# All 22 units of the up projection in seven block products, four of them begun in an order written by hand; a tail laid out anew; a modulation vector turned earlier

## The chip, the cores and the metric

The kernel runs on one core of a Trainium2 chip. A core has five engines that work side by side and wait for one another by semaphores: TensorE (PE: matrix products into the accumulator memory PSUM), VectorE (DVE), ScalarE (ACT), GpSimd (POOL) and SyncE (SP), which issues most transfers between HBM and the on-chip memory SBUF. The metric is the device time of one execution in microseconds (us); less is better.

## The reference, cut to what matters

One layer of a diffusion backbone over 1024 tokens of width 1024: a combined projection, neighbourhood attention, two-way retention, gated merge, an output projection and a residual; then a gated MLP with a short convolution along the tokens. The change is in the MLP, at its entrance and at the kernel's end:

```python
x = x + g1 * _merge(o_na, o_ret, xga, xgb, w_proj_na, w_proj_ret, w_out)
hx2 = _rmsnorm(x, norm2_g) * (1.0 + sc2) + sh2
u = hx2 @ w_up                                   # 1024 x 5632
u = sum(up[:, i:i + n] * conv_w[i] for i in range(3)) + conv_b
a, val = split(u, 2)
x = x + g2 * ((silu(a) * val) @ w_down)          # 2816 x 1024
return _rmsnorm(x, final_norm_g)
```

Everything is float32. The kernel makes a float32 product of three matmuls: each operand is split into a rounded high part (ACT, a copy to the type float32r) and the rest (DVE, a subtraction), and high by high, high by low and low by high are added in PSUM.

## The kernel before, in words

**Units.** The up projection's 5632 columns are worked as 22 units. A unit is one block of 128 gate columns together with its 128 value columns, over all 1024 tokens: a 2 x 2 grid of output blocks (two branches by two halves of 512 tokens), summed over 1024 inputs, which are two groups of four blocks of 128. Done plainly (`up`, with `mm_a`), a unit takes 2 branches x 2 halves x 8 input blocks x 3 = 96 matmuls of 128x512. Done in seven block products (class `Seven`, for this stage its subclass `Up`), it takes 7 x 4 x 3 = 84: the weights' 2 x 2 blocks a11, a12, a21, a22 and four sums s1 to s4 of them are multiplied by B11, B21, B22 and four sums T1 to T4 of the moving blocks (the products T2 and T1 with s2 and s1, T3 with s3, T4 with a22), and DVE combines the products. In the kernel before, the first two units (`PLAIN = 2`) are plain and the other 20 go by seven products. `open3` (L1417) issues the matmuls of the seven-product units, `chain` (L117 to L119) those of the plain ones.

**Where the operands come from.** `out_proj(tb)` computes 128 tokens of the residual stream into `xr`; `norm_out(tb)` turns `xr` on PE (row `tp`), applies scale and shift (the vector `a2` and a part of `col`) and leaves high and low parts: for the first half of the tokens in `h2a`, for the second in `h2h` and `h2l`. For the tokens of the second half it also forms the four sums T1 to T4 with the first half's rows (`vo`, read back from `d_h`) and stores them in `d_t`. They are loaded again and split into the tiles `T` (16 splits of 128x512), which the seven-product units need. Eight blocks of tokens are done one after another; `norm_out` of a block comes behind `out_proj` of the next.

**Weights.** Each weight block is loaded into one of 12 raw buffers (`ur`; `raw` ahead of that stage) and split into one of six buffers `wc`. For the first units of the seven products the sums s1 to s4 are made in HBM by adding DMAs that POOL issues during the gates stage and `out_proj` (`block_sums`, `puts`, into `d_s`: six units, 48 DMAs); for later units POOL adds them in SBUF.

**What sets the order.** Outside blocks under `tc.manual_schedule()` a scheduler orders each engine's instructions; inside them they stand as written. Each engine works its own list in order. In the seven-product stage the units are interleaved: sorted by 7 x unit + 2 x step, so two units are open at a time. `conv` (three taps, silu, product) follows a unit's last combination on ACT and DVE. The down projection (`y` banks) ends the program; its last four bank results are finished one after another under a manual order (`finish`: factor on POOL, scaling on ACT and DVE, two stores).

**The second modulation vector.** Behind the 16 `pn` products, `col[:, 16:48]` (shift, scale and gates) is added to its bias, turned on PE into `tpa`, copied by ACT to `arow` and stored in `d_ada`, from where gate rows are read back.

Of the kernel before, what the change touches and what calls it, by code (L numbers as in the profile page):

```python
# [40 lines left out]
def tile_hybrid_layer(ctx, tc: tile.TileContext, io, dbg=None):  # L41
# [17 lines left out]
    d_s = dram.tile([6, 4, P, 512], F32, name="d_s")  # L59
# [490 lines left out]
    NH, PLAIN, PRE = NF // 2, 2, 6  # L550
# [28 lines left out]
    def up_jobs():  # L579
        return weight_jobs(d_s, [io["w_up"][seq[PLAIN + n]] for n in range(PRE)])  # L580
# [838 lines left out]
    class Seven:  # L1419
# [14 lines left out]
        def prod(self, bank, a, c, first, last):  # L1434
            w = wtile()
            split(w[:, 0], w[:, 1], a)
            for k, (xh, xl) in enumerate(self.moving(c)):
                open3(bank, w[:, 0, k * P : (k + 1) * P], w[:, 1, k * P : (k + 1) * P], xh, xl, first and k == 0, last and k == KH - 1)
# [97 lines left out]
    hs = None  # L1536
    hs = [hx_sums(k) for k in range(KH)]
# [9 lines left out]
    for n, (db, half) in enumerate(order):  # L1547
# [25 lines left out]
    pool.tensor_tensor(col[:, 16:48], col[:, 16:48], bcol[:, 16:48], ALU.add)  # L1573
    a2 = cpool.tile([P, KB], F32, name="a2")
    pool.tensor_scalar(a2, col[:, 32:40], 1.0, None, ALU.add)
    pool.tensor_tensor(a2, a2, gcol[:, 1], ALU.mult)
    tpa = g_ps("tpa")
    pe.transpose(tpa[:32, :P], col[:, 16:48], ident)
    arow = ap_.tile([32, P], F32, name="arow")
    act.copy(arow, tpa[:32, :P])  # L1580
    sync.dma_start(d_ada, arow)
# [137 lines left out]

    def norm_out(tb, xr):  # L1720
        half, ts = tb // 4, slice((tb % 4) * P, (tb % 4 + 1) * P)
        if tb == 4:
            h2[1] = [(gtile(0, F32R, "h2h"), gtile(0, F32R, "h2l")) for _ in range(KB)]
        vr = op.tile([P, KB, P], F32, tag="v", bufs=2, name="v")
        if half:
            vo = op.tile([P, KB, P], F32, tag="vo", bufs=1, name="vo")
            sync.dma_start(vo, d_h[tb - 4])
        for kg in range(2):
# [3 lines left out]
            for k in range(4):  # L1732
                kb = kg * 4 + k
                t = h2[half][kb]
                h_, l_ = (t[:, 0, ts], t[:, 1, ts]) if half == 0 else (t[0][:, ts], t[1][:, ts])
                a, sh = a2[:, kb : kb + 1], col[:, 24 + kb : 25 + kb]
                act.activation(h_, tp[:, k], AF.Identity, bias=sh, scale=a)
                v = vr[:, kb]
                vec.tensor_scalar(v, tp[:, k], a, sh, ALU.mult, ALU.add)
# [5 lines left out]
        (b11, b21), (b12, b22) = [(t[:, : KB // 2], t[:, KB // 2 :]) for t in (vo, vr)]  # L1745
# [7 lines left out]
    xr = None  # L1753
    for tb in range(NTB):
        nx = out_proj(tb)
        if tb < NTB - 2:
            puts(up_sums, nx[:, 0:1], 3)
        if tb:
            norm_out(tb - 1, xr)
        xr = nx  # L1760


    def up(u, wu, half):
        h = h2[half]
        hi, lo = ([t[:, i] for t in h] if half == 0 else [t[i] for t in h] for i in range(2))
        mm_a(u[:, half * 512 : half * 512 + 512], wu, lambda k: hi[k], lambda k: lo[k])

    def up_load(j, br):
        return [wload(io["w_up"][j, br, i]) for i in range(2)]

    def u_tile(n):
        return pu[n // 2 % 2].tile([P, T], F32, tag="u", bufs=2, name="u")

    for _ in up_sums:
        pass
    early = []
    for br in range(2):
        early.append((u_tile(br), up_load(0, br)))
        up(*early[br], 0)
    norm_out(NTB - 1, xr)  # L1780
    po.release()
    pu.append(ps("u_ps1", "left"))
    op.release()
    wop.release()
    gpool[1].release()


    rp = sb("raws", "right")
    tpl = sb("combs", "right")
    tap = sb("conv", "right")  # L1790
# [253 lines left out]
    with tc.manual_schedule():  # L2044
        tl = [operands(6, j) for j in range(NH - NL, NH)]
        for b in range(QB):
# [11 lines left out]
            if b:  # L2058
                finish(b - 1, 1)
# [113 lines left out]
```

## Time and profile before

| | us |
|---|---|
| median of three runs (lowest, highest) | 1724.81 (1722.7, 1724.94) |
| the profiled execution: its time, its span | 1725.1, 1723.3 |
| PE busy | 1705.5 (99%) |
| DVE busy | 1225.8 (71%) |
| ACT busy | 823.5 (48%) |
| POOL busy | 578.4 (34%) |
| granted TensorE clock, mean | 0.998 |

A matmul's busy time in the profile is longer than the distance between two of them, since they overlap; what one costs in a row of many is the group's busy time by its count. In a group row, the numbers behind the bar are the group's busy time, the mean length of one, the idle time of its engine just before, and what ended that. In a row of the windows, each engine's busy time is followed by its number of instructions, then the granted clock, the share of the DMA engines and GB/s. `u` is a PSUM bank of the up projection, `h2l` the low part of the second half's input, `T` a split sum, `wc` a split weight block.

### The profile page before, as it was taken

To read this page: it belongs to the slowest core of one execution; us is meant where nothing else is said; L and a number is where in the kernel's file an instruction comes from. 1 tells how busy PE (TensorE), PEld (TensorE's weight loads), DVE (VectorE), ACT (ScalarE), POOL (GpSimd) and SP (SyncE) were. 2 spreads that over 40 slices of the span, in tenths; PEclk is the share of its full clock that TensorE was granted. 3 is DMA by queue.
4 is the path that set the end of the run, shared out by engine and by line. 5 is a ranking of instruction groups with operands and counts; after the bars stand their busy time and mean duration, and the time that the engine had idled before them with its cause. 6 is when DMAs were issued, how large, how long until landed. Compare 5 with 4: busy or idle time off the path is not lost.

```text
span 1723.3 us, 25172 instructions
## 1 busy us (share of the span) xinstructions
PE 1705.5 (99%) x8425; PEld 1421.9 (83%) x8425; DVE 1225.8 (71%) x2437; ACT 823.5 (48%) x1733; POOL 578.4 (34%) x756
## 2 busy tenths in 40 slices
PE   9999999999999999999999999999999999999998
PEld 7788888888888887888888888788888888888886
DVE  5777786665787877565564567867888888856756
ACT  6565665553453444443453334544444444544444
POOL 2112234223334443013222121013666566421444
PEclk9999999999999999999999999999999999999999
DMA  9356779853353523888984666867566766998744
GB/s 380 93 151 161 179 200 241 201 129 91 82 155 82 172 59 110 298 287 255 300 260 156 202 194 193 278 213 213 165 172 185 197 187 171 263 313 291 244 154 176
DMA packets 165474, 338.24 MB, mean 196 GB/s; under 512 B 29408, under 2 KB 46336, under 8 KB 159136
## 3 DMA queue, kind: packets, MB, share of 16 engines
q1 hardware_dynamic: 130448, 240.83, 41.5%
q0 software_dynamic: 20288, 80.86, 22.3%
q10 hardware_dynamic: 14608, 14.95, 2.6%
q8 instruction: 66, 1.08, 0.3%
q14 instruction: 64, 0.52, 0.1%
HBM read 261.27 MB, written 136.63 MB: 231 GB/s over the span
## 4 chain that ended last, share of the span: by engine, by line
PE 40%; issue 5%; DVE 5%; DMA 4%; POOL 2%; ACT 2%; POOLq 0%; ACTq 0%; SPq 0%; DVEq 0%
PE u L1417 27%; PE y L1417 2%; PE pr L117 2%; PE pr L118 2%; PE pr L119 2%; DMA ur<-d_a 2%; PE om L130 1%; PE om L128 1%; PE om L129 1%; DMA ur<-in_w_down 1%; DVE ta L1822 1%; DVE ta L1823 1%; POOL x L1982 1%; DMA vo<-d_h 1%; PE u L118 1%
## 5 line engine op out<-in xcount | busy, mean ns | idle before, releaser
L1417 PE MATMUL u<-T,wc 128*128 128x512 f32 x960 | 225.3, 390 | 1.1 <-ACT pu L1451 0.9
L1417 PEld LDWEIGHTS u<-T,wc 128*128 128x128 f32 x960 | 179.4, 188 | 41.6 <-ACT pu L1451 4.3
L1417 PE MATMUL y<-wc,ahl 128*128 128x512 f32 x924 | 210.1, 389 | 0.4 <-DVE wc L94 0.4
L1417 PEld LDWEIGHTS y<-wc,ahl 128*128 128x128 f32 x924 | 173.4, 188 | 36.8 <-DVE wc L94 0.8
L94 DVE TENSOR_TENSOR wc<-ur,wc 128x512 fp32r<-128x512 f32 x161 | 118.9, 742 | 63.4 <-ACT wc L93 63.4
L93 ACT CAST wc<-ur 128x512 fp32r<-128x512 f32 x161 | 99.7, 621 | 118.9 <-PE u L1417 73.6
L118 PE MATMUL mm<-low,wc 128*128 128x512 f32 (+1 forms) x312 | 119.1, 382 | 0.0
L1417 PE MATMUL u<-h2a,wc 128*128 128x512 f32 x480 | 113.3, 390 | 0.3 <-DVE pu L1460 0.2
L117 PE MATMUL mm<-hx,wc 128*128 128x512 f32 x264 | 107.3, 407 | 0.2 <-ACT hc L231 0.2
L1417 PEld LDWEIGHTS u<-h2a,wc 128*128 128x128 f32 x480 | 89.6, 188 | 20.7 <-issue 1.8
L119 PE MATMUL mm<-hx,wc 128*128 128x512 f32 x264 | 104.9, 397 | 0.0
L532 POOL DMA_DIRECT2D d_ona<-rs x32 | 33.1, 1035 | 204.7 <-DMA d_ona<-rs 61.1
L588 POOL COPY pad<-pu 128x1 f32<-128x1 f32 x54 | 36.7, 680 | 189.9 <-DVE pu L1454 149.9
L1417 PE MATMUL u<-hxT,wc 128*128 128x512 f32 x384 | 89.8, 389 | 0.0
L1417 PEld LDWEIGHTS u<-hxT,wc 128*128 128x128 f32 x384 | 72.1, 188 | 14.9
L93 ACT CAST wc<-raw 128x512 fp32r<-128x512 f32 x84 | 52.0, 622 | 46.4 <-PE pr L119 9.8
L94 DVE TENSOR_TENSOR wc<-raw,wc 128x512 fp32r<-128x512 f32 x84 | 61.3, 734 | 12.4 <-ACT wc L93 9.8
L93 ACT CAST wc<-s 128x512 fp32r<-128x512 f32 x56 | 34.8, 622 | 71.3 <-PE u L1417 67.0
L130 PE MATMUL mm<-wc,low 128*128 128x512 f32 (+1 forms) x180 | 68.9, 383 | 0.0
L93 ACT CAST wc<-wr 128x512 fp32r<-128x512 f32 x56 | 34.7, 620 | 64.3 <-PE u L1417 44.1
L118 PEld LDWEIGHTS mm<-low,wc 128*128 128x128 f32 x312 | 59.1, 190 | 7.2
L1417 PE MATMUL u<-hx,wc 128*128 128x512 f32 x192 | 62.2, 390 | 0.6 <-ACT arow L1580 0.6
(415 smaller groups left out, 4748.6 us busy)
## 6 DMA issues: line engine op xcount, KB each, us to landing
d_a<-at SPq DMA_DIRECT2D x77, 256.0 KB, 5.4
ur<-d_a SPq DMA_DIRECT2D x77, 256.0 KB, 5.3
ur<-in_w_up SPq DMA_DIRECT2D x74, 256.0 KB, 6.7
d_w<-in_w_down POOLq DMA_DIRECT2D x66, 256.0 KB, 7.0
aw<-in_w_ada SPq DMA_DIRECT2D x32, 512.0 KB, 4.3
d_a<-d_a POOLq DMA_DIRECT2D x44, 256.0 KB, 7.4
ur<-d_w SPq DMA_DIRECT2D x44, 256.0 KB, 3.8
d_s<-in_w_up POOLq DMA_DIRECT2D x36, 256.0 KB, 6.0
```

The lines of the kernel that those rows point to most:

```text
L93: act.copy(hi, src)
L94: (lo_eng or vec).tensor_tensor(lo, src, hi.bitcast(F32), ALU.subtract)
L117: pe.matmul(out, wh, xh, start=k == 0, stop=False)
L118: pe.matmul(out, wh, xl, start=False, stop=False)
L119: pe.matmul(out, wl, xh, start=False, stop=k == n - 1)
L128: pe.matmul(out, ah, bh, start=first, stop=False)
L129: pe.matmul(out, ah, bl, start=False, stop=False)
L130: pe.matmul(out, al, bh, start=False, stop=last)
L532: late(pool.dma_start(o, self.rs[HD:P], accum_op=ALU.add))
L588: late(pool.tensor_copy(tick, src))
L1417: pe.matmul(out, a, b, start=first and n == 0, stop=last and n == 2, skip_group_check=True)
L1822: vec.scalar_tensor_tensor(dst[:, 1:T], u[:, 0 : T - 1], cw[:, blk, 0:1], dst[:, 1:T], ALU.mult, ALU.add)
```

## The change

- `PLAIN = 2` goes; all 22 units go by seven products. The sums of the first eight units (`PRE = 8`) are now made in HBM, 64 DMAs instead of 48; in the gates stage POOL issues two after step 2 of a unit as well.
- The first four units (class `Opening`) begin with those products that need no T: units 0 and 1 with B11, B21 and B22, units 2 and 3 with B11 and B21. That is ten products. Their results are kept (`p1`, `zs`, `cs` or the unit's own `uu` tile), and what is left of these units (class `Later`) is four products for units 0 and 1 and five for units 2 and 3. In units 0 and 1 the B22 product is closed on its own and kept in `zs`; POOL adds u2 to it (L1928).
- The opening stands in a manual order: turning the last token block, loads, splits, sums, keeps and T splits are placed by hand among the ten products, up to the first two T products of unit 0.
- `norm_out` of the second half no longer leaves high and low parts of input blocks 0 to 3 (only plain units used these); ACT makes their `v`, DVE that of blocks 4 to 7. `vo` is read in halves for four token blocks at once into other buffers.
- PSUM banks of the up projection are single ones, four to a pool, instead of pairs.
- `second_cols` (the vector's turning) is called at `pn` product 8 of 16.
- At the end, the last bank's last four weight groups run as two halves of 256 columns (24 matmuls for 12), each half combined and squared on its own; the block ahead of it is scaled behind that.

```diff
-    NH, PLAIN, PRE = NF // 2, 2, 6
+    NH, EARLY, PRE = NF // 2, 4, 8
...
+        if n == 8:
+            second_cols()
...
-        if k in (1, 3):
-            puts(up_sums, (gu[i].u2 if k == 1 else gu[i].u3)[:, 0:1], 2)
+        if k in (1, 2, 3):
+            puts(up_sums, (gu[i].u3 if k == 3 else gu[i].u2)[:, 0:1], 2)
...
                 kb = kg * 4 + k
+                a, sh = a2[:, kb : kb + 1], col[:, 24 + kb : 25 + kb]
+                v = vr[:, kb]
+                if half and kb < KH:
+                    act.activation(v, tp[:, k], AF.Identity, bias=sh, scale=a)
+                    continue
+                vec.tensor_scalar(v, tp[:, k], a, sh, ALU.mult, ALU.add)
...
-    for n, j in enumerate(seq[:PLAIN]):
-        us2 = []
-        for br in range(2):
-            u, wu = (u_tile(2 * n + br), up_load(j, br)) if n else early[br]
-            for half in range(2) if n else (1,):
-                up(u, wu, half)
-            us2.append(u)
-        for c in ((1, 0), (2, 3))[n]:
-            combs[f"T{c + 1}"] = comb(c)
-        conv(j, *us2)
...
+    with tc.manual_schedule():
+        o0.prod(0)
+        o0.keep_p()
+        o1.prod(0)
+        o1.keep_p()
...
+        o0.prod(1)
+        for kg in (1, 0):
+            for k in range(4):
+                pe.transpose(tps7[kg][:, k], xr[:, (4 * kg + k) * P : (4 * kg + k + 1) * P], ident)
+        o1.prod(1)
...
+        comb_load(1, 3)
+        comb_load(0, 0, 1, 2)
+        o2.prod(0)
+        o0.prod(2)
+        o2.keep_p()
+        o2.prod(1)
+        o3.split(0)
+        o1.split(2)
+        comb(1, 0, 1, 2)
+        o3.split(1)
+        comb_load(0, 3)
+        o0.keep(uu_tile())
+        o1.keep(uu_tile())
+        o3.prod(0)
+        o0.keep_z()
+        o2.keep()
+        comb(1, 3)
+        o1.prod(2)
+        o3.keep_p()
+        comb(0, 0, 1)
+        o3.prod(1)
+        u0 = Later(o0)
+        u0.load()
+        comb_load(2, 0, 1, 2, 3)
+        comb(0, 2, 3)
+        u0.s2 = u0.weights(u0.s2)
+        o1.keep_z()
+        u0.s1 = u0.weights(u0.s1)
+        comb(2, 0, 1)
+        u0.step(0)
+        o3.keep()
+        comb_load(3, 0, 1, 2, 3)
+        comb(2, 2, 3)
+        u0.step(1)
+    comb(3, 0, 1, 2, 3)
...
+            last = b == QB - 1
+            parts = (slice(0, 256), slice(256, 512)) if last else (slice(0, 512),)
+            for c in parts:
+                for i, (a, w) in enumerate(tl):
+                    open3(banks[0][b][:, c], a[:, 0, ts], a[:, 1, ts], w[:, 0, c], w[:, 1, c], False, i == NL - 1)
```

How the instructions stand now is shown at three places. First PE, from the turning of token block 6 onward. Before, with the last matmul of unit 0's first half ahead of the turning of block 7 (`tp`) and the second half's first matmuls behind it:

```order
L119 MATMUL u<-h2a,wc 128x512
L1731 MATMUL tp_11905<-ident,xn 128x128 x4
L1731 MATMUL tp_11922<-ident,xn 128x128 x4
L117 MATMUL u<-h2h,wc 128x512 x2
L118 MATMUL u<-h2l,wc 128x512
L119 MATMUL u<-h2h,wc 128x512
```

and now (`wu` are weight blocks kept outside the `wc` buffers):

```order
L1743 MATMUL tp_11831<-ident,xn 128x128 x4
L1417 MATMUL u<-h2a,wc 128x512 x12
L1417 MATMUL u<-h2a,wu 128x512 x12
L1417 MATMUL u<-h2a,wc 128x512 x12
L1974 MATMUL tp_11891<-ident,xn 128x128 x4
L1974 MATMUL tp_11890<-ident,xn 128x128 x4
L1417 MATMUL u<-h2a,wu 128x512 x12
L1417 MATMUL u<-h2a,wc 128x512 x12
L1417 MATMUL u<-h2h,wc 128x512
L1417 MATMUL u<-h2l,wc 128x512
```

Between the turning of block 7 and the first use of the second half's input there stood nothing; now two products of 12 matmuls stand there, and three, not four times twelve, ahead of the turning.

Second DVE, from its last operation on token block 7's input to the first T splits. Before:

```order
L1739 TENSOR_SCALAR v<-tp_11922,a_8886,col 128x128
L1746 TENSOR_TENSOR vo<-vo,v 128x512
L1740 TENSOR_TENSOR h2l<-v,h2h 128x128
L1747 TENSOR_TENSOR v<-v 128x512
L94 TENSOR_TENSOR wc<-raw,wc 128x512
L1748 TENSOR_TENSOR v<-v,vo 128x512
L1749 TENSOR_TENSOR vo<-vo,v 128x512
L94 TENSOR_TENSOR wc<-raw,wc 128x512
L94 TENSOR_TENSOR T_12016<-ur,T_12015 128x512 x4
L94 TENSOR_TENSOR T_12034<-ur,T_12033 128x512
L1822 SCALAR_TENSOR_TENSOR ta<-u,cw,ta 128x1023
```

and now:

```order
L2019 TENSOR_SCALAR vr<-tp_11891,a_8509,col 128x128 x4
L2022 TENSOR_TENSOR vo<-vo,vr 128x512
L2023 TENSOR_TENSOR vt<-vr,vo 128x512
L2025 TENSOR_TENSOR h2l<-vr,h2h 128x128 x4
L94 TENSOR_TENSOR wc<-ur,wc 128x512
L2027 TENSOR_TENSOR vt<-vr 128x512
L2028 TENSOR_TENSOR vo<-vo,vt 128x512
L94 TENSOR_TENSOR wc<-ur,wc 128x512 x2
L94 TENSOR_TENSOR T_11937<-ur,T_11936 128x512 x3
```

The convolution of a plain unit (L1822) is gone from among the T splits; weight splits of units 1 to 3 have come in ahead of them.

Third ACT, at the passage from the opening into the interleaved units, as it is now (T_11938 is T1's tile, T_11940 T3's, T_11942 T4's; `zs` and `cs` are kept results):

```order
L1805 COPY pu<-u 128x512
L93 CAST T_11938<-ur 128x512 x4
L93 CAST wc<-ur 128x512
L1809 COPY zs<-u 128x512
L93 CAST wc<-ur 128x512
L93 CAST T_11940<-ur 128x512 x2
L1814 COPY cs<-u 128x512
L93 CAST T_11940<-ur 128x512 x2
L93 CAST wc<-ur 128x512
L93 CAST T_11942<-ur 128x512 x4
```

Copies that wait for a PE product (`pu`, `zs`, `cs`) now stand among the splits, which on this engine wait behind them.

More of the change, by code (lines that the diff above doesn't have):

```diff
@@ L1751, in norm_out @@
             sync.dma_start(d_t[c, tb - 4], t)
[L1753 to L1769, printed above, removed]
@@ L1917, in tile_hybrid_layer @@
-    dn_sums = block_sums(down_jobs(0, NH))
-    for i, n in interleaved(PLAIN, NF):
-        units[i].step(n)
-        if n in (1, 3) and i > PLAIN:
+    opening = [Opening(n) for n in range(EARLY)]
+    o0, o1, o2, o3 = opening
+    xr = None
+    for tb in range(NTB):
+        if tb == NTB - 1:
+            o0.load(rawload, 0, 1)
+            o0.split(0)
+            o0.split(1)
+            o1.load(rawload, 0)
+            o1.split(0, "wu")
+            o1.load(rawload, 1)
+            o1.split(1, "wu")
+        nx = out_proj(tb)
+        if tb < NTB - 2:
+            puts(up_sums, nx[:, 0:1], 3)
+        if tb:
+            norm_out(tb - 1, xr)
+        xr = nx
@@ L1921, in tile_hybrid_layer @@
+    for _, i, n in sorted(order):
+        if i or n > 1:
+            units[i].step(n)
+        if n in (1, 3) and i >= EARLY - 1:
             puts(dn_sums, (units[i].u2 if n == 1 else units[i].u3)[:, 0:1], 2)
```

260 lines of the change are left out of this document (186 added, 74 removed).

## The prediction

> **What bounds the kernel now.** I read the page's busy times first, then the busy time by stage, then PE's waits. PE is the bound:
>
> ```profile
> PE 1705.5 (99%) x8425; PEld 1421.9 (83%) x8425; DVE 1225.8 (71%) x2437; ACT 823.5 (48%) x1733; POOL 578.4 (34%) x756
> ```
>
> Of the span of 1723.3 us PE leaves 17.8 us. A matmul taken off PE is therefore worth its full distance, if nothing else becomes late there. In the windows the third row is the stage of the two plain units, the fourth the first three seven-product units, the last the steady stage:
>
> ```profile
> core 0: us, PE busy (x) PEld busy (x) DVE busy (x) ACT busy (x) POOL busy (x), PEclk, DMA share, GB/s
> 740.00:980.00 240.00, 240.00 (x1061) 198.76 (x1060) 135.17 (x198) 99.89 (x166) 60.72 (x86) 1.00 0.76 246
> 1072.30:1118.80 46.50, 45.37 (x203) 36.86 (x202) 39.29 (x77) 27.10 (x47) 0.86 (x1) 1.00 0.81 275
> 1118.80:1176.00 57.20, 57.20 (x253) 47.23 (x253) 39.75 (x50) 25.02 (x37) 10.86 (x16) 1.00 0.70 207
> 1233.00:1500.00 267.00, 265.84 (x1163) 217.14 (x1163) 232.98 (x242) 122.54 (x169) 161.62 (x161) 1.00 0.71 196
> ```
>
> PE is full everywhere; in the plain units' stage it loses 46.50 - 45.37 = 1.13 us. DVE is the second bound: 39.29 of 46.50 (84%) there, 87% in the steady stage. PE's waits that the change touches are:
>
> ```profile
> PE u L118 <- DVE h2l L1740: 1.0, 2, 0.7
> PE u L1417 <- ACT pu L1451: 0.9, 5, 0.2
> PE u L1417 <- ACT arow L1580: 0.6, 1, 0.6
> ```
>
> The first is the plain unit waiting for token block 7's low parts, the third the gates waiting behind the vector's turning. The second belongs to the steady stage, whose order stays.
>
> **Removed matmuls.** Two units go from 96 to 84 matmuls: 24 fewer. The distance of one is the busy time of a long row by its count:
>
> ```profile
> L1417 PE MATMUL y<-wc,ahl 128*128 128x512 f32 x924 | 210.1, 389 | 0.4 <-DVE wc L94 0.4
> ```
>
> 210.1 / 924 = 0.227 us, so -24 x 0.227 = **-5.45 us**. The mean of 389 ns is not the price, since matmuls overlap. (Against this the Trainium skill, "TensorE: Matmul & The Clock Gate", Back-to-back issue gap, gives about 131 ns for a matmul of 512 columns in a sustained stream with weight loads, by which the sum would be an estimated -3.1 us. The trace disagrees: 227 ns over 924 of them, and the measurement decides.)
>
> **The handoff into the opening.** Count from the end of block 6's turning. A product of 12 matmuls takes 2.72 us, eight turnings 0.87 us. Split times and the rest of the ledger come from:
>
> ```profile
> 1012.50 0.87 PE tp L1731 x8
> L94 DVE TENSOR_TENSOR T<-ur,T 128x512 fp32r<-128x512 f32 x16 | 10.1, 684 | 2.3 <-ACT T L93 2.3
> L93 ACT CAST T<-ur 128x512 fp32r<-128x512 f32 x16 | 9.0, 619 | 3.4 <-DMA d_t<-vo 3.3
> L1739 DVE TENSOR_SCALAR v<-tp,a,col 128x128 f32<-128x128 f32 x24 | 9.1, 403 | 0.0
> L1740 DVE TENSOR_TENSOR h2l<-v,h2h 128x128 fp32r<-128x128 f32 x24 | 6.1, 281 | 0.0
> L1737 ACT ACTIVATE h2h<-tp,col,a 128x128 fp32r<-128x128 f32 x24 | 10.2, 454 | 11.2 <-DVE v L1739 5.6 <-PE tp L1731 5.3
> L1746 DVE TENSOR_TENSOR vo<-vo,v 128x512 f32<-128x512 f32 x3 | 2.1, 687 | 3.0 <-DMA vo<-d_h 3.0
> L1451 ACT COPY pu<-u 128x512 f32<-128x512 f32 x15 | 8.5, 567 | 0.0
> ur<-d_t SPq DMA_DIRECT2D x16, 256.0 KB, 4.5
> ```
>
> A split costs ACT 9.0 / 16 = 0.56 and DVE 10.1 / 16 = 0.63 us. PE reaches block 7's turning at 8.2, is through it at 9.0, and needs block 7's high and low parts at 9.0 + 2 x 2.72 = 14.5. DVE and ACT can have them some 4 us behind the turning (ACT's four `v` and four casts at 10.2 / 24 = 0.43 each, DVE's two sums of 0.69 and four low parts of 0.25): near 13. So two products cover what waited 1.0 us before. That wait goes: **-1.1 us** with its remainder.
>
> What is late next are three later handoffs, on ACT, whose splits stand behind copies that wait for PE. The eighth product ends at 22.7; then ACT copies it (0.57), splits T1 four times, splits s2: 26.1, DVE 26.8, and unit 0's first T product starts at 28.1. Cover 1.3. Two more copies, s1, four splits of T3 and s3 bring ACT to about 30.5; DVE does s3, u2 (0.69, behind PE's 30.8) and two T3 splits: about 33.1, and PE needs T3 at 33.5. Cover 0.4. Four T4 splits and unit 1's s2 end on DVE at about 36.2, and PE needs s2 at 36.3. Cover about nothing. Their raw tiles come by SP, which runs its queue in order behind `d_t` stores, and take 4.5 us each; unit 1's s2 can only be loaded when DVE frees a buffer at about 31, so it lands at about 35.5, on the edge. These waits share one cure: once PE has waited, all later cover grows. The bound below is 0. Above I take 3.0 us, the longest that a load was late in this stage (row L1746). The nearest row for PE itself is its single longest wait, 0.7; I take **+0.7 us**.
>
> **DVE over the whole opening.** Four low parts and four `v` less in each of four token blocks: 16 x (6.1 / 24 + 9.1 / 24) = 10.1 us less. More: six splits (14 for 8) at 0.63, 3.8 us, and five combinations in each of two units at 0.69, 6.9 us: 10.7. Even, so DVE's share stays near 84%. But it is spread unevenly: units 0 and 1 now leave four products, 10.9 us of PE, and cost DVE a convolution (four taps and a product), five combinations and four splits. By these rows, from the stage without POOL additions,
>
> ```profile
> L1822 DVE SCALAR_TENSOR_TENSOR at<-uu,cw,at 128x1023 f32<-128x1023 f32 x2 | 2.6, 1284 | 1.3 <-ACT at L1821 1.3
> L1831 DVE SCALAR_TENSOR_TENSOR at<-ta,at 128x1024 f32<-128x1024 f32 x2 | 2.4, 1222 | 0.0
> L94 DVE TENSOR_TENSOR wc<-ur,wc 128x512 fp32r<-128x512 f32 x24 | 16.3, 688 | 7.4 <-ACT wc L93 7.4
> L1454 DVE TENSOR_TENSOR pu<-pu,u 128x512 f32<-128x512 f32 x3 | 2.1, 686 | 1.8 <-PE u L1417 1.7
> ```
>
> that is 4 x 1.28 + 1.22 + 9 x 0.69 = 12.5 us, 1.6 over. I cost it at 0: PE waits for splits and combinations, not for the convolution, whose outputs are used only in the down projection; six `wc` buffers let the splits run up to five products (13.6 us) ahead; and the seven-product units give time back (7 x 2.72 = 19.1 us each against 87% of DVE). Without that cover it is 2 x 1.6 = +3.2 us.
>
> **Sixteen more adding DMAs, 10 more on SP, a third issue per gates unit.** POOL is busy 60.72 of 240 us in the gates and DMA 0.76; 16 x 256 KB on some 59 MB is 7%. PE, which issues without a gap there, covers it: 0; if an operand came late once, up to 1.
>
> **The vector's turning.** In the middle of the `pn` products ACT's copy has other banks ahead of it, and PE does not stop: **-0.6 us** (between -0.6 and 0; the turning itself only moves).
>
> **The tail.** Behind PE's last matmul came, for 512 columns, two DVE steps and a square:
>
> ```profile
> 1714.91 0.69 DVE L2055 TENSOR_TENSOR z<-y,gate 128x512 f32<-128x512 f32 x1 [0.64 <-PE y L1417]
> 1715.64 0.69 DVE L2056 TENSOR_TENSOR z<-pd,z 128x512 f32<-128x512 f32 x1
> 1716.43 0.63 ACT L1977 ACTIVATE xr<-z 128x512 f32<-128x512 f32 x1 [1.38 <-DVE z L2056]
> 1718.18 0.75 DVE L1990 SCALAR_TENSOR_TENSOR z<-z,ssf,fg 128x512 f32<-128x512 f32 x1 [1.19 <-POOL ssf L1987]
> L1249 DVE TENSOR_TENSOR o<-O,o x32: 409/416/425, 440.6 to 687.7; 128x256 f32<-128x256 f32 x32
> L520 PE MATMUL R<-PT,V 128*128 128x256 f32 x304 | 47.9, 284 | 0.9 <-DVE PT L505 0.8
> ```
>
> With 256 columns DVE saves 2 x (0.69 - 0.42) = 0.55, the square some 0.2 by the same proportion. Block 2's scaling now also stands behind the last square, in time that POOL's factor takes anyway. Twelve matmuls of 512 (2.73) become 24 of 256: at least half of 0.227 each (+0), at most 47.9 / 304 = 0.158 (+1.05); that row has other work between, so I take +0.25. Tail: **-0.5 us** (-0.8 to +0.3).
>
> **Sum.** -5.45 - 1.1 + 0.7 - 0.6 - 0.5 = -6.95 us. The profiled execution took 1725.1, so 1718.15; it stood 0.3 above the median of 1724.81, so **1718.0 us** with rounding, 0.4% faster. About 0.2% (3.4 us) is what a measurement of this kernel can tell from no change: faster ends at 1721.4, slower begins at 1728.3.
>
> **The rivals.** *The handoffs stall in earnest.* ACT's order puts splits behind copies, and cover is nearly nil at T3 and unit 1's s2. If each of two loads is late by 3.0 us and PE waits for both, +6.0 in place of +0.7: about 1723, no change that can be told. For it: the ledger's thin cover, 4.5 us a load at 0.81 DMA share. Against: in the kernel before, T loads were 3.3 us late for ACT and PE waited for none of them; and the first wait gives cover to the second, so one at 3.0 (1720.3) is the commoner form. Chance 0.22 for both forms, half of it above 1721.4.
>
> *DVE becomes the bound in units 0 to 3.* If combinations queue behind convolution steps so that DVE's excess reaches PE, the price at quiet rates is +3.2: 1721.2, chance 0.06. It ends slower if DVE also runs there at the rates of the steady stage, where POOL adds at the same time:
>
> ```profile
> L1822 DVE SCALAR_TENSOR_TENSOR ta<-uu,cw,ta 128x1023 f32<-128x1023 f32 x16 | 28.6, 1785 | 10.1 <-ACT ta L1821 10.1
> L1823 DVE SCALAR_TENSOR_TENSOR ta<-uu,cw,ta 128x1023 f32<-128x1023 f32 x16 | 27.0, 1688 | 0.0
> L94 DVE TENSOR_TENSOR wc<-s,wc 128x512 fp32r<-128x512 f32 x56 | 51.9, 928 | 0.5
> ```
>
> Then a four-product unit costs DVE 1.79 + 1.69 + 2 x 1.28 + 2.04 + 5 x 0.69 + 4 x 0.93 = 15.3 us against 10.9, a five-product unit 16.2 against 13.6: 2 x 4.4 + 2 x 2.6 = +14.0, 1732 us. It decides from about 7 us on. For it: two POOL additions (`zs`) are new there. Against: two of them reach a few DVE steps; the four-addition groups of POOL begin with unit 8, as before. Chance 0.04. (The Trainium skill, "SBUF — State Buffer", Who interferes with whom, says a DVE instruction with two SBUF inputs blocks against a GpSimd one that reads SBUF; the rows above, 1785 against 1284 ns, agree.)
>
> *Only the count counts:* the waits at the vector and the tail move elsewhere and give nothing, -5.85: 1719.3. Chance 0.10.
>
> **How the numbers follow.** The forecast with its own range (stall 0 to 2, tail and vector in their bounds: 1716.5 to 1719.5) has 0.58. The range is 1715.5 to 1722.0: below, every term at its best (-5.45 - 1.1 - 0.6 - 0.8 gives 1716.9) and the spread of the runs shown, above, one full stall or the quiet DVE excess. Faster: 0.58 + 0.10 + half of 0.22 + 0.03 = 0.82; slower 0.05 (0.04 and a little of the stalls); same 0.13.
>
> **What would show it.** In the new profile PE should have 12 instructions fewer, and about 5.2 us less busy time. Right: the waits for `h2l` and `arow` are gone, and PE has at most about 1 us of waits between the last `om` and unit 4, for `wc` or T splits. If there are several waits of over 1 us for `wc` or T splits ended by a DMA or ACT, the first rival holds; if they fall in units 1 to 3 with DVE full and its steps over 1.5 us, the second. The last PE matmul to the end of the span should shrink from 8.4 to about 7.7 us. A clock below 1.00, or a gap in the gates stage, would make the prediction wrong from a side that I gave no price.

## The result, and the profile after

Six runs of each kernel gave a median of 1714.07 us (1711.22 to 1718.05) for the changed kernel and 1723.76 us (1721.08 to 1726.28) for the kernel before. The ratio is 0.9946, with a 95% interval from 0.9935 to 0.9957. The forecast was 1718.0 us with a range from 1715.5 to 1722.0. The direction was right, but the gain is 9.7 us instead of 7, and 1714.07 lies below the range. The profiled execution of the changed kernel took 1713.59 us, with a span of 1711.8.

First the busy times of the page:

```profile
PE 1696.4 (99%) x8413; PEld 1418.8 (83%) x8413; DVE 1224.5 (72%) x2423; ACT 832.1 (49%) x1749; POOL 595.0 (35%) x783
```

PE has the 12 instructions fewer that were forecast (8425 before), but its busy time fell by 9.1 us where 5.2 were expected. Since it is as full as before (99%), something that had counted as busy has gone beside the removed matmuls.

PE's waits in the changed kernel's up projection, from the list of waits:

```profile
PE tp L1974 <- ACT h2h L1754: 0.3, 1, 0.3
PE u L1417 <- DVE T L94: 0.2, 1, 0.2
```

The waits for `h2l` and `arow` are gone, and what is new sums to 0.5 us. So far the prediction holds. But the five waits for `pu` L1451 in the steady stage, which the prediction left in place, are gone as well. The windows show what that is worth; the first row is of the kernel before, the second of the changed one:

```profile
1233.00:1490.00 257.00, 255.84 (x1120) 209.14 (x1120) 224.03 (x231) 117.90 (x163) 159.25 (x157) 1.00 0.71 192
```

```profile
1233.00:1490.00 257.00, 257.00 (x1135) 212.80 (x1134) 228.59 (x237) 122.01 (x171) 160.03 (x159) 1.00 0.71 196
```

In the same 257 us PE issued 1120 matmuls before and 1135 after, 15 more: 15 x 0.2275 = 3.4 us. The busy column shows only 1.16 us of that.

To find where the time went, I took the starts of PE's matmuls from the trace and cut the program at five of them. "Late starts" is, for neighbouring matmuls, the distance between their starts beyond 0.2275 us (0.088 for a turning), summed where it is above 0.06. "Opening" is from the last `om` to 1118 us, "steady" from there to the last `u`. Where six `y` matmuls stand among the last `u`, their 1.4 us are counted with the down projection. All in us:

| | before | after |
|---|---|---|
| start to first `pn` (nothing changed) | 694.31 | 694.80 |
| first `pn` to first gate matmul | 44.78 | 44.03 |
| first gate matmul to last `om` | 332.21 | 332.19 |
| last `om` to last `u` | 433.05 | 422.15 |
| of this late starts, opening (the opening of before had 2.66 in b_single, below) | 2.07 | 1.18 |
| of this late starts, steady | 4.26 | 0.29 |
| last `u` to last `y` | 210.15 | 210.38 |
| last `y` to the last scaling | 4.44 | 4.49 |
| the last store behind it | 4.35 | 3.76 |

The sum is 11.5 us between these two executions, more than the 9.7 between the medians: the profiled execution of before stood 1.3 us above its median, that of the changed kernel 0.5 below. Of the 10.9 us in the up projection the 24 matmuls are 5.46, the opening 0.9, the steady stage 4.0; the remaining 0.6 are delays below 0.06 us each, which gather around the late starts. The steady stage is the largest term that the prediction lacked.

### The profile page after: what moved, and what is told of

Read it like the earlier page. It is cut to its first block, busy times and chain, and to the rows that moved or that the text cites. A ratio compares the mean times of both kernels' runs of the same rounds, so it can differ in the third digit from the quotient of the medians.

```text
span 1711.8 us, 25236 instructions
## 1 busy us (share of the span) xinstructions
PE 1696.4 (99%) x8413; PEld 1418.8 (83%) x8413; DVE 1224.5 (72%) x2423; ACT 832.1 (49%) x1749; POOL 595.0 (35%) x783
## 4 chain that ended last, share of the span: by engine, by line
PE 81%; DMA 5%; issue 5%; DVE 4%; POOL 3%; ACT 1%; SPq 0%; POOLq 0%; ACTq 0%; DVEq 0%
PE u L1417 31%; PE mm L130 4%; PE mm L128 4%; PE mm L129 4%; PE mm L118 4%; PE mm L119 4%; PE mm L117 4%; PE y L1417 2%; PE R L520 2%; PE ptp L502 2%; DMA ur<-in_w_down 2%; PE pr L118 2%; PE pr L117 2%; PE pr L119 2%; DMA ur<-d_a 2%
## 5 line engine op out<-in xcount | busy, mean ns | idle before, releaser
L1417 PE MATMUL u<-T,wc 128*128 128x512 f32 x1056 | 246.4, 389 | 0.3 <-DVE T L94 0.2
L1417 PEld LDWEIGHTS u<-T,wc 128*128 128x128 f32 x1056 | 198.0, 188 | 42.4 <-DVE T L94 0.6
L1417 PE MATMUL y<-wc,ahl 128*128 128x512 f32 (+1 forms) x936 | 210.1, 386 | 0.4 <-DVE wc L94 0.4
L94 DVE TENSOR_TENSOR wc<-ur,wc 128x512 fp32r<-128x512 f32 x171 | 126.8, 745 | 49.0 <-ACT wc L93 49.0
L93 ACT CAST wc<-ur 128x512 fp32r<-128x512 f32 x171 | 105.7, 622 | 110.4 <-PE u L1417 57.1
L1417 PE MATMUL u<-h2a,wc 128*128 128x512 f32 x504 | 118.3, 389 | 0.0
L1417 PEld LDWEIGHTS u<-h2a,wc 128*128 128x128 f32 x504 | 94.5, 188 | 19.6
L94 DVE TENSOR_TENSOR ahl<-ur,ahl 128x512 fp32r<-128x512 f32 x66 | 52.5, 801 | 22.0 <-ACT ahl L93 21.8
L93 ACT CAST wc<-raw 128x512 fp32r<-128x512 f32 x78 | 48.5, 622 | 39.0 <-PE pr L119 9.8
L94 DVE TENSOR_TENSOR wc<-raw,wc 128x512 fp32r<-128x512 f32 x78 | 57.2, 738 | 11.8 <-ACT wc L93 9.3
```

The lines of the kernel that those rows point to most:

```text
L93: act.copy(hi, src)
L94: (lo_eng or vec).tensor_tensor(lo, src, hi.bitcast(F32), ALU.subtract)
L1417: pe.matmul(out, a, b, start=first and n == 0, stop=last and n == 2, skip_group_check=True)
```

## The experiments

**The steady stage: who keeps PE waiting.** In the kernel before, the chain of waits has this piece, and six more like it between 1207 and 1445 us (start, us, what):

```profile
1280.68 0.70 DVE uu L1441
1281.46 1.25 ACT ta L1821
1282.74 2.75 DVE ta L1822
1285.49 0.60 DVE pu L1460
1286.09 1.64 DVE ta L1823
1287.82 1.06 ACT ta L1824
1288.88 0.48 ACT pu L1451
1289.40 30.23 PE u L1417 x132
```

It goes through a unit's convolution (`ta`) on DVE and ACT. ACT's copy `pu` of the next unit's X bank (L1451) stands behind ACT's convolution step, which waits for DVE; and PE's product behind it, into Y, starts 0.04 us after the copy. The data of that product, s2 times T2 into Y, do not need the copy. What X and Y have in common is that they are the two halves of one PSUM tile. The same holds for DVE's `pu` L1460, which reads Y, and the product B21, which goes into X. From this the theory: the tile that X and Y share makes the waits, and the change's single banks removed them. The rival: the opening shifts convolutions, POOL's additions and transfers against the products, so that nothing is late any more.

Experiment b_single takes the kernel before and changes only the banks of the seven-product units:

```diff
-            t = u_tile(2 * self.n)
-            self.X, self.Y = t[:, 0:512], t[:, 512:1024]
-            self.Z = u_tile(2 * self.n + 1)[:, 0:512]
+            self.X, self.Y, self.Z = (u_bank(self.n) for _ in range(3))
...
+    pu[1].release()
+    pu[0].release()
+    pu = [ps("u_ps2", "right"), ps("u_ps3", "left")]
+    def u_bank(n):
+        return pu[n % 2].tile([P, 512], F32, tag="u", bufs=4, name="u")
     units = [Up(n, j) for n, j in enumerate(seq)]
```

> The kernel before, with one thing of the change: from the first seven-product unit on (unit 2), X, Y and Z of a unit are three PSUM tiles of one bank each, where before X and Y were the halves of one tile of two banks. Both plain units, the vector's turning, the tail and the number of matmuls stay as before. Theory (the pair tile): in the profile of before PE starts a product late at ten places between 1211 and 1444 us, always a product into Y behind one into X's copy, or one into X behind DVE's reading of Y; the late starts sum to 4.3 us. The waits come from the shared tile and not from the data, so they go: 4 us faster (1719.5 to 1720 us, ratio 0.9976), units of 84 matmuls at 19.04 us throughout. Rival (the gain of the steady stage came from elsewhere: another phase of the convolutions, of POOL's additions or of the transfers against the products, which the opening shifts): no change, late starts still sum to 3 us or more.

Measured: 1720.35 us against 1723.05 of the kernel before, ratio 0.9983 (0.9974 to 0.9992). By the medians that is 2.7 us (1.4 to 4.5 by the interval), less than the 4 expected. In the trace the steady stage has no late start, and the last `om` to the last `u` takes 428.73 us for 433.05. Its chain of waits there is one piece:

```profile
1120.24 369.93 PE u L1417 x1632
```

Experiment a_pairs is the reverse: the changed kernel with the pair tile from unit 4 on.

```diff
-            self.X, self.Y, self.Z = (u_bank(self.n) for _ in range(3))
+            t, z = (pu[self.n % 2].tile([P, T], F32, tag="u", bufs=2, name="u") for _ in range(2))
+            self.X, self.Y, self.Z = t[:, 0:512], t[:, 512:1024], z[:, 0:512]
```

> The changed kernel, with one thing put back: from unit 4 on X and Y of a unit are again the halves of one PSUM tile of two banks; the opening, the vector, the tail and the number of matmuls are the change's. Theory (the pair tile): late starts come back in the steady stage, some 3 to 5 us in sum: 1717 to 1719 us, ratio to before about 0.997. Rival (the gain came with the new phase of the opening): stays at 1714, ratio 0.9946.

Measured: 1718.0 us, ratio 0.9968 (0.9957 to 0.9978). The late starts of the steady stage are back with 2.78 us (0.29 in the changed kernel), a little under the 3 to 5 expected; this execution's opening also lost 1.8 us more than the changed kernel's, of which more below. The chain is back too:

```profile
1394.75 0.60 DVE pu L1464
1395.35 1.64 DVE ta L1838
1397.08 1.06 ACT ta L1839
1398.14 0.48 ACT pu L1455
1398.66 30.26 PE u L1417 x132
```

Both directions agree, so the pair tile is the cause, and the rival falls. One thing is not separated: with single tiles a unit holds three of its pool's four banks, where the pairs held all four and left one unused, so a spare bank came with them. Against the spare bank as the cause stands what ended the listed waits of before: a reader of the other half of the tile that PE writes next, `pu` L1451 or `pu` L1460. The rows of the weight loads had shown the waits better than those of the matmuls. Of the kernel before, of b_single and of a_pairs (behind the second bar the idle time before them, and what ended most of it):

```profile
L1417 PEld LDWEIGHTS u<-T,wc 128*128 128x128 f32 x960 | 179.4, 188 | 41.6 <-ACT pu L1451 4.3 <-ACT uu L1890 0.2
```

```profile
L1417 PEld LDWEIGHTS u<-T,wc 128*128 128x128 f32 x960 | 180.2, 188 | 37.4
```

```profile
L1417 PEld LDWEIGHTS u<-T,wc 128*128 128x128 f32 x1056 | 197.4, 188 | 45.0 <-ACT pu L1455 2.9 <-DVE T L94 0.6 <-issue 0.4
```

PE's matmul rows gave `pu` L1451 0.9 us in five waits; the weight loads give it 4.3 in eight. That shows the waits but does not price them: by the starts of the matmuls, the products into Y behind `pu` L1451 lost 3.0 of the stage's 4.26 us, and the other products 1.25. The reason why the matmul rows show so little is the one that the page states for itself: ends of matmuls are modelled. A matmul of 0.39 us that is issued every 0.2275 covers the first 0.16 us of every wait.

**The vector's turning.** Experiment a_turn puts the call of `second_cols` back behind the last `pn` product.

```diff
-        if n == 8:
-            second_cols()
...
     gu[0].load()
+    second_cols()
```

> The changed kernel with the modulation vector's turning back behind the last pn product. The prediction priced its move at 0.6 us. In the trace the distance from the last pn matmul to the first gate matmul was 1.26 us before and 0.34 after, but PE reached the last pn 0.65 us later in the changed kernel's profile. If 0.6 is right, the wait for arow returns with 0.6 us and the first gate matmul comes 0.6 us later; rival: PE gets to the first gate matmul at the same time, because what the gates' first product waits for is something else.

Measured: 1715.73 us (three runs), ratio 0.9949 (0.9934 to 0.9964), which alone tells nothing against the changed kernel's 0.9946. The trace tells more. The wait is back:

```profile
PE u L1417 <- ACT arow L1550: 0.6, 1, 0.6
```

From the first `pn` matmul to the first gate matmul it takes 44.80 us, as in the kernel before (44.78) and in b_single (44.81); in the ten traces with the early turning it takes 44.02 to 44.04. So the move is worth 0.77 us: the listed wait of 0.6 and the 0.16 that a matmul's modelled end covers of it.

**The tail.** Experiment a_tail is the changed kernel with the last block in one piece.

```diff
-            parts = (slice(0, 256), slice(256, 512)) if last else (slice(0, 512),)
+            parts = (slice(0, 512),)
...
-            if last:
-                factor(b - 1, 1)
...
-            if last:
-                scaled(b - 1, 1)
-            elif b:
+            if b:
                 finish(b - 1, 1)
-        factor(QB - 1, 5)
+        factor(QB - 1, 1)
```

> The changed kernel with the tail of before: the last block in one piece of 512 columns. The prediction priced the new tail at -0.5 us (+0.25 for matmuls of 256 columns, -0.75 behind the last matmul). In the two profiles the last matmul to the end was 8.80 us before and 8.26 after, and the down stage was 0.24 us longer: -0.3 in sum. Expected: behind the last matmul 8.8 us again, the down stage 0.24 us shorter. Rival: the tail's end hangs on the DMA out, and the end stays at 8.3.

Measured: 1715.27 us (two runs), ratio 0.9951 (0.9933 to 0.9969). From the last `u` to the last `y` 210.19 us (210.38 with halves), from there to the last scaling 4.44 (4.49 with halves), the last store 3.92. So neither what I expected (8.8 us behind the last matmul; it was 8.36) nor the rival (8.3 because of the store) is quite it: in calculation the halves lose 0.24 us in all, and the store has a part of its own in the difference. DVE's timeline in the changed kernel says why the halves gain nothing:

```profile
1702.34 0.74 DVE L2155 SCALAR_TENSOR_TENSOR z<-z,ssf,fg 128x512 f32<-128x512 f32 x1
1703.88 0.42 DVE L2230 TENSOR_TENSOR z<-y,gate 128x256 f32<-128x256 f32 x1 [0.79 <-PE y L1417]
1704.34 0.42 DVE L2231 TENSOR_TENSOR z<-pd,z 128x256 f32<-128x256 f32 x1
1704.68 0.42 DVE L2230 TENSOR_TENSOR z<-y,gate 128x256 f32<-128x256 f32 x1
1705.13 0.43 DVE L2231 TENSOR_TENSOR z<-pd,z 128x256 f32<-128x256 f32 x1
```

PE's last matmul starts at 1703.56. Only then does DVE begin the first half, which PE had finished twelve matmuls (1.4 us) earlier, so all four short steps lie behind the end. Both halves are columns of one tile in one bank. The Trainium skill ("PSUM — Partial Sum Buffer", PSUM bank collisions raise a hardware error) says that accesses by two engines must be kept apart by bank, not by address. That bears on both findings: here the halves share a bank, and the wait is one that the rule asks for; X and Y of a unit were different banks, and b_single agrees that their waits were not needed.

**The opening.** a_turn, a_tail and a_pairs share the change's opening but lost more in it than the changed kernel's profile: late starts of 3.75, 4.21 and 2.97 us for 1.18. PE's timeline in a_tail has three waits, of which the profile of the changed kernel has only the second:

```profile
1078.74 3.02 PE L1417 MATMUL u<-h2a,wc 128*128 128x512 f32 x12 [1.07 <-ACT pu L1805]
...
1082.53 0.66 PE L1974 MATMUL tp<-ident,xn 128*128 128x128 f32 x4 [0.33 <-ACT h2h L1754]
...
1089.92 0.50 PE L1417 MATMUL u<-h2l,wc 128*128 128x512 f32 x1 [1.03 <-DVE h2l L2025]
```

The copy `pu` and the high parts `h2h` stand on ACT behind the square of block 7, and that waits for DVE, which is late with blocks 6 and 7 altogether. In DVE's timeline of the changed kernel, and of a_tail, the place is:

```profile
1057.52 0.69 DVE L1764 TENSOR_TENSOR vo<-vo,v 128x512 f32<-128x512 f32 x1
1061.96 0.69 DVE L94 TENSOR_TENSOR wu<-raw,wu 128x512 fp32r<-128x512 f32 x1 [3.74 <-DMA d_t<-vo]
1062.57 0.68 DVE L1719 TENSOR_TENSOR xn<-om,gate 128x512 f32<-128x512 f32 x1
```

```profile
1063.31 0.69 DVE L94 TENSOR_TENSOR wu<-raw,wu 128x512 fp32r<-128x512 f32 x1 [5.47 <-DMA d_t<-vo]
```

`wu` is the first weight of opening unit 1 (`o1.split(0, "wu")`). The raw weight has landed; its low part is to go into a buffer from which a `vo` is still being stored to `d_t`. DVE stands there until the store has read it, and behind it in DVE's order are block 6's second output half and all that follows. Four runs tell whether that is the cause; the first is the changed kernel once more.

> The changed kernel as it is, once more, beside the next three. In the two experiments whose opening is the change's own, PE lost 1.5 to 2.1 us at the products o0.prod(1) and o2/o0.prod(2) (waits for the copy pu and for h2l) that the changed kernel's first profile does not show. Theory (a thin handoff that stalls in most executions): this profile shows such waits too, 1.5 us or more from the last om to unit 0's first T product, and the median stays near 0.9946. Rival (the extra waits belong to those two kernels): none here, 0.3 us or less.

a_again measured 1713.73 us (1713.08 to 1715.43), ratio 0.9946 (0.9934 to 0.9959). By the measure of the expectation, the listed waits for `pu` and `h2l` (1.5 us in a_turn, 2.1 in a_tail), it shows 0.4 us: well short of the 1.5, and nearer to the rival. The late starts, which that list partly hides, decide more: 2.25 us in the opening, of which 1.0 are at those two places, where the changed kernel's first profile has none. So the extra loss does occur in the changed kernel itself and varies from execution to execution. The opening's late starts were 1.18, 2.25, 2.97, 3.75 and 4.21 us where DVE stood 3.7, 4.5, 4.7, 5.6 and 5.5 us at `wu` (the changed kernel, a_again, a_pairs, a_turn, a_tail): more with more standing, but for the last two.

DVE waits for a store a second time on the same path. Directly ahead of block 7's low parts, DVE's sum `vt` waits for a store of `vo`; in a_tail:

```profile
1088.97 0.69 DVE L2023 TENSOR_TENSOR vt<-vr,vo 128x512 f32<-128x512 f32 x1 [1.65 <-DMA d_t<-vo]
```

In the same order of runs DVE stands there 0.27, 0.74, 1.22, 0.99 and 1.65 us, and the first products that need `h2l` lose 0, 0.4, 0.9, 0.7 and 1.3 us by their starts. The two rank the five runs alike, and the second wait would explain why a_tail lost more than a_turn. No run takes this wait away alone.

a_late pins `wu` behind block 7's first output half. In its trace this is the one instruction of DVE there that changes place; on ACT the copy of unit 1's second weight comes three high parts later, in time that ACT waited anyway. The edit:

```diff
+            if dh == 0:
+                mid()
...
-            o1.split(0, "wu")
-            o1.load(rawload, 1)
-            o1.split(1, "wu")
-        nx = out_proj(tb)
+        nx = out_proj(tb, o1.split_late if tb == NTB - 1 else lambda: None)
+        if tb == NTB - 1:
+            o1.load(rawload, 1)
+            o1.split(1, "wu")
...
+        def split_late(self):
+            self.w[0] = hi, lo = [gtile(0, F32R, "wu") for _ in range(2)]
+            act.copy(hi, self.raw[0])
+            late(vec.tensor_tensor(lo, self.raw[0], hi.bitcast(F32), ALU.subtract))
```

> The changed kernel with one VectorE instruction moved: the low half of opening unit 1's first weight (tile wu) is formed behind block 7's first output half instead of ahead of block 6's second. Its buffer is the one from which block 4's combination vo is stored to d_t; in the traces VectorE stands 3.7 us (changed kernel) and 5.5 us (old tail) at that instruction until the store has read it, with the scaling, norms and turnings of blocks 6 and 7 queued behind. Theory (that wait is what starves the opening): VectorE does not stand there any more, block 7's normalised rows are ready 3 us earlier, and PE's waits for pu L1805, h2l and the second turning's bank go: 0.3 us faster than the best opening seen and 1.5 to 2.5 us faster than the changed kernel's median (ratio to before 0.9935). Rival (the handoff is short of ScalarE and VectorE time as such): the waits stay within 0.5 us, ratio 0.9946.

Measured: 1712.11 us (1711.42 to 1713.06), ratio 0.9936 (0.9923 to 0.995), 1.6 us below a_again beside it. DVE no longer stands at `wu`, and block 6's second half follows when PE has it, 3.0 us earlier (3.89 by the clock, less the 0.94 by which this execution is ahead already at the first `pn`):

```profile
1056.57 0.69 DVE L1766 TENSOR_TENSOR vo<-vo,v 128x512 f32<-128x512 f32 x1
1058.68 0.69 DVE L1719 TENSOR_TENSOR xn<-om,gate 128x512 f32<-128x512 f32 x1 [1.42 <-PE om L130]
```

The waits for `pu`, for the second turning's bank and for `h2l` are gone, and late starts of 0.65 us are left in the opening. The theory holds in mechanism and size. DVE still stands 0.94 us at `vt`, but forms it 2.5 us earlier than in a_again, and `h2l` is ready when PE needs it.

a_24 lengthens the cover instead: the first products of units 0 and 1 are computed twice.

```diff
         o0.prod(0)
+        o0.again()
         o0.keep_p()
         o1.prod(0)
+        o1.again()
```

> The changed kernel with 24 matmuls more: the first sum-free product of opening units 0 and 1 is computed twice, the second time over the first (the result stays). If a matmul is worth its full distance, 24 x 0.227 = +5.45 us. If the opening stalls behind blocks 6 and 7, the doubled products also cover the handoff, and up to 2 us of waits go: +3.4 to +5.45, with the waits for pu L1805 and h2l gone. Rival (PE's count is not what sets the stage): less than +2.

Measured: 1718.27 us, ratio 0.9972 (0.9961 to 0.9982), 4.5 us above a_again. The waits for `pu` and `h2l` are gone although DVE stood 3.4 us at `wu`. Against a_late, where the handoff does not wait either, the last `om` to the last `u` is longer by 427.59 - 421.61 = 5.98 us, of which 0.54 are new late starts at T splits; the rest is 5.44 us for 24 matmuls, 0.227 each. The price of a matmul was right. (By the Trainium skill's 131 ns, "TensorE: Matmul & The Clock Gate", Back-to-back issue gap, they would have cost an estimated 3.1; the measurement decides.)

a_best is a_late with the tail of a_tail.

> a_late with the tail of before (the last block in one piece of 512 columns). In the profiles the change's tail gained nothing in calculation: from PE's last matmul to the last scaling 4.49 us against 4.44 before, since both halves of the last block lie in one PSUM bank and VectorE starts on the first half only when the second is finished; and 24 matmuls of 256 columns cost 0.23 us more than 12 of 512. Theory: 0.2 to 0.3 us faster than a_late in the stages, within the noise of the median. Rival (the halves do help): slower than a_late by 0.5 us.

Measured: 1711.52 us (1711.38 to 1714.94), ratio 0.9937 (0.9925 to 0.995). In its stages the old tail saves 0.20 in the down projection and 0.05 in calculation, and the last store takes 3.95 us for 3.74: it gives nothing in sum, as expected within the noise. What was left was to try whether two of the change's own parts, the halves and the T3 handoff, could be made to gain.

**Its own bank for the second half.** a_bank is a_late with the last four steps of the second half's columns in a bank of their own; what the first bank already holds is scaled and taken off ahead of time.

```diff
+            ys = [banks[0][b][:, c] for c in parts]
+            if last:
+                ys[1] = pd[1].tile([P, 512], F32, tag="y", bufs=4, name="y")[:, 0:256]
...
-                vec.tensor_tensor(z[:, c], banks[0][b][:, c], gate2[:, 512 + c.start : 512 + c.stop], ALU.mult)
+                vec.tensor_tensor(z[:, c], ys[n], gate2[:, 512 + c.start : 512 + c.stop], ALU.mult)
...
+            if b == 1:
+                c, q = slice(256, 512), dw_tile("xr", 4)
+                vec.tensor_tensor(q[:, c], banks[0][QB - 1][:, c], gate2[:, 768:1024], ALU.mult)
+                vec.tensor_tensor(p1[QB - 1][:, c], p1[QB - 1][:, c], q[:, c], ALU.subtract)
```

> a_late with one difference in the tail: the second half of the last block's columns puts its last four steps into a PSUM bank of its own (what the first bank already holds of it is scaled and taken off on VectorE earlier). The result stays. Theory (the halves gain nothing because they share a bank): VectorE's two steps of 0.43 us on the first half now run while PE makes the second, and from PE's last matmul to the last scaling it takes about 4.49 - 0.86 = 3.6 us. Rival (POOL's chain of three steps sets the end): stays within 0.2 us of 4.49.

Measured: 1711.87 us (1711.72 to 1712.33), ratio 0.9931 (0.9918 to 0.9945). From the last `y` to the last scaling 3.69 us instead of 4.49. DVE's timeline, with PE's last matmul at 1702.50:

```profile
1701.34 0.75 DVE L2162 SCALAR_TENSOR_TENSOR z<-z,ssf,fg 128x512 f32<-128x512 f32 x1
1702.01 0.42 DVE L2240 TENSOR_TENSOR z<-y,gate 128x256 f32<-128x256 f32 x1
1702.46 0.43 DVE L2241 TENSOR_TENSOR z<-pd,z 128x256 f32<-128x256 f32 x1
1702.82 0.42 DVE L2240 TENSOR_TENSOR z<-y,gate 128x256 f32<-128x256 f32 x1
```

DVE begins the first half without a wait, ahead of PE's end. So it was the sharing that kept it back. Whether by tile or by bank a_bank does not tell, since it gives the second half a tile and a bank of its own at once. The median is 0.24 us below a_late's, too near to tell; the 0.8 us are read from the stage.

**T3 earlier.** The one late start of the opening that is left in a_late is at T3, with 0.47 us:

```profile
1105.33 1.89 PE L1417 MATMUL u<-T,wc 128*128 128x512 f32 x7 [0.20 <-DVE T L94]
```

Unit 0's u2 stands ahead of the last two T3 splits on DVE and waits for PE's product. a_t3 puts the splits first:

```diff
-        comb(2, 0, 1)
+        comb(2, 0, 1, 2, 3)
         u0.step(0)
         o3.keep()
         comb_load(3, 0, 1, 2, 3)
-        comb(2, 2, 3)
         u0.step(1)
```

> a_late with one difference in the opening's order: the last two splits of T3 stand ahead of unit 0's first T product, not behind VectorE's combination that waits for that product's end. Theory: the start that is late by 0.47 us at T3's first low part (1105.3 us in a_late's trace) goes, the stage from the last om to the last u shrinks from 421.6 to 421.1 us. Rival (T3's raw tiles land too late): unchanged, or a wait as long at another split.

Measured: 1711.38 us (1711.28 to 1711.49), ratio 0.9928 (0.9914 to 0.9941); the stage takes 420.68 us, 0.93 less than in a_late. Twice what was expected, mostly because the small late start at 1133 us (0.32) has gone too; late starts of 0.18 us are left in the whole up projection.

> a_late with both: the second half's own bank in the tail and the early splits of T3. Expected by the sum of the two: 0.5 + 0.86 = 1.3 us less than a_late, some 1711 us, ratio to before 0.993; if neither holds, 0.9936 as a_late.

a_both measured 1710.54 us (1709.97 to 1711.53), ratio 0.9924 (0.9911 to 0.9938): 1.6 us less than a_late's median, and with the stages as in the two (420.68 and 3.70). Its median lies 3.2 us below the changed kernel's in the run beside a_late, though in another set of runs; against the kernel before it gains 13 us where the change gained 9.4.

## Why the prediction was right and wrong

| term | predicted | measured |
|---|---|---|
| 24 matmuls | -5.45 | -5.46 |
| steady stage | 0 | -4.0, and most of 0.6 in small delays |
| opening: `h2l` wait, new stalls | -1.1 + 0.7 | -0.9 in the first profile, +0.2 to +2.1 in the four others |
| vector's turning | -0.6 | -0.77 |
| tail, calculation and matmuls | -0.5 | +0.3 |
| last store | not priced | -0.6 |

**Wrong: the steady stage.** The step that failed is "The second belongs to the steady stage, whose order stays". The order did stay; the dependences did not. The list of changes has the single banks in it, and the prediction gave them no price and no sentence. The signs were in rows that it quotes: five waits for `pu` L1451 behind a product that needs no `pu`, and 1163 matmuls in 267 us, which at 0.227 fill only 264. So the term that was put at 0 measured some -4: -4.3 us of up projection between the traces of b_single and the kernel before, -2.7 (-1.4 to -4.5) between their medians. Added to 1718.0 that gives 1713.7 or 1715.3; the first is within 0.4 of the median. That it comes so near is in part luck: the other errors nearly cancel, and the opening alone varies by 3 us from execution to execution. "PE is full everywhere" overlooked the same stage: the steady row that stands there leaves 267.00 - 265.84 = 1.16 us idle.

**Right: the count.** 24 matmuls at 0.227 us; a_24 gives 5.44 for 24 back. **Right in mechanism, a little small: the vector.** 0.77 instead of 0.6, since the list of waits leaves out what a matmul's modelled end covers.

**Partly right: the handoffs.** Of the three thin covers that were named, T3's was late (0.47 us with a forecast cover of 0.4); at T2 and s2, and at unit 1's s2, nothing waited. The larger loss was at a place that was not named: "two products cover what waited" counted busy times from block 6's turning on, and did not ask when DVE gets to block 6 at all. What the change had put into DVE's order ahead of that, a split into a buffer that is still being stored, cost 3.7 to 5.6 us of DVE and, with the second store at `vt` behind it, 0.5 to 3.6 us of PE (late starts of 1.18 to 4.21, less the 0.65 of a_late; the smallest in the first profile). The 3.0 us that the prediction took for the longest lateness of a load are a sum of two waits, 2.79 and 0.22. So the first rival, handoffs that stall, came true in part, with another mechanism than late loads. It did not turn the result, because the steady stage gave more.

**Wrong: the tail.** "DVE saves 2 x (0.69 - 0.42) = 0.55" assumed that the first half is worked while PE makes the second. It is not, in one tile of one bank (a_bank: 0.8 us better with two). The 24 short matmuls cost 0.2 as forecast (0.25):

```profile
L1417 PE MATMUL y<-wc,ahl 128*128 128x256 f32 x24 | 3.0, 283 | 0.0
```

The last matmul to the end did shrink, from its end 8.41 to 7.98 us where 7.7 was forecast, but by the store, and not by what the prediction said.

**The other rivals.** DVE did not become the bound in units 0 to 3: between 1118 and 1233 us its busy time rose from 85.7 to 96.1 of 114.2 us, and PE had late starts of 0.29 there. "Only the count counts" was right for the tail, which gave nothing, and wrong for the vector (a_turn: 0.77 us).

## What to carry to other kernels

When a change alters how buffers are cut (a pair tile into single banks, a tile name that takes over another's buffers), list every instruction that waited on the old tile and every one that will wait on the new one, and price that apart from the order of the work. Look for short waits of PE in the idle time of its weight loads, and price them by the starts of its matmuls or their number per window, not by its busy time. And a wait that stands in an in-order queue costs what is queued behind it: a low part of a weight, needed 13 us later, and a second store behind it cost PE up to 3.6 us.

## What the runs showed of the hardware that was not expected

A wait of PE costs more than its row says. At the nine clear late starts of the steady stage before, six of which are listed with 0.2 us at most, the start is late by 0.26 to 0.35 us (the modelled end covers 0.16 of it), and the start after it by another 0.08 to 0.11: some 0.4 us for a listed 0.2. Matmuls of 256 columns follow one another every 0.120 us, little more than half of the 0.2275 of 512 columns, with a weight load each.

The last store, from the last scaling to the end of the span, took 4.33 to 4.35 us in the two traces without the change's opening (the kernel before and b_single), 3.73 to 3.76 in those with opening and halved tail, and 3.92 to 3.95 in the two with the opening and the old tail. That is a sixteenth of the gain, and I have no cause for it; no run was made on it.
